# Middle feed-forwards of a two-layer decoder trunk: one group of columns, seven block products in the output projection, and some modulation dots beside the mixing stage

## The chip, the cores and the metric

The kernel runs as one launch on one core of a Trainium2 chip. The metric is the device time of a launch in microseconds (us). A core has five engines with their own instruction queues, each worked through in order: TensorE (PE, matmuls; its weight loads are listed as PEld), VectorE (DVE), ScalarE (ACT), GpSimd (POOL) and SyncE (SP). In this kernel SP issues the plain DMA loads and POOL the loads that add to what already lies in the destination, and the loads of the modulation weights. Matmul results land in PSUM; everything else lies in SBUF.

## The reference

The hidden state h has 512 tokens by 1024 features, in float32. There are two layers, and each is a half-step feed-forward, a mixing stage, and a second half-step feed-forward. Every one of the six stages begins with an RMS norm that is scaled and shifted by values made from a conditioning vector c, and ends with a residual that is gated by such values.

```python
c_act = silu(c)
for l in range(2):
    mod = c_act @ w_ada[l] + b_ada[l]          # 9 vectors of 1024: shift, scale, gate, three times
    hn = rms_norm(h, g_ffn1[l]) * (1 + sc1) + sh1
    gate, up = split(hn @ w_ffn1_in[l])        # 1024 -> 2 x 2816
    h = h + 0.5 * (1 + gt1) * ((silu(gate) * up) @ w_ffn1_out[l])    # 2816 -> 1024
    hn = rms_norm(h, g_mix[l]) * (1 + sc2) + sh2
    h = h + (1 + gt2) * (concat(attention, rwkv7, short_conv)(hn @ w_mix_in[l]) @ w_mix_out[l])
    # the second feed-forward is like the first, with w_ffn2_in, w_ffn2_out, sh3, sc3, gt3
```

## The kernel before

**Layout and precision.** h lies transposed: eight tiles `h[i]` of 128 features by 512 tokens. `HALVES` names the two halves of the tokens, `lo_` (0 to 255) and `hi_` (256 to 511). A product in float32 is made from three matmuls: each operand is split into a high part (`wH`, a cast on ACT, L104) and a low part (`wL`, the remainder, a subtraction on DVE, L105), and high times high, high times low and low times high are summed (`mm3`, `mm6`, `prod`). So each block of weights that PE multiplies costs ACT one cast and DVE one subtraction of the same size first. Four buffers each hold `wH` and `wL`.

**The order of the stages** is ffn1, mix and ffn2 of layer 0, then the same of layer 1 (`seq`, L1365). In this document the first feed-forward is ffn1 of layer 0, the *middle* ones are ffn2 of layer 0 and ffn1 of layer 1, and the *last* one is ffn2 of layer 1. All are made by `ffn` (L372), in these phases:

- *First tiles.* The first pairs of 128-wide columns of gate and up (two pairs, `n_first`; four in the first feed-forward) come from plain products with `w_in`.
- *Pairs* (`pair_in`, L483). Every further pair of columns is made by seven block products in place of eight, in the manner of Strassen and Winograd. Sums of quarters of hn (`P1`, `P2`, `T3`, `T4`, made in `whole` and `combine` beside the first tiles) meet sums of blocks of weights. The weight sums are made as follows: `S` is one block loaded by SP and a second added on top by a POOL load; DVE then adds block A(0,0) (`a11`, L497) and later subtracts, by sign, A(0,1) (L524); `S3`, the third pair sum, is A(0,0) loaded a second time into the tile `third` (L525) with A(1,0) added by a POOL load. Each product is 24 matmuls of 256 columns. Results are copied from PSUM to SBUF (`up`, `s1`, `s2`), added there (`gate` from `pG` and `s1`, L521), and put through silu and the product with up. The last product of a pair, `rest`, is done in the middle of the next pair.
- *Output product.* In the first and middle feed-forwards the 22 blocks of 128 inner columns go in two `GROUPS` of 12 and 10. After the pairs of each group come plain products with `w_out` over the group: 8 outputs of 128 features, 512 tokens wide, three matmuls each (L783); the last two outputs of the second group run by halves in `close` (L323), where the next stage's norm is worked in: `stats`, `spread` and `apply` of the lo half, then of the hi half, with the order on DVE and ACT written out by hand. The next stage's first three tiles start with the lo half.
- In the last feed-forward (`whole_k`) there is one group, and the output product itself is made by seven block products (`out_strassen`, L546): 42 `units`, seven products by six pieces of the inner columns; the gate is applied and h updated (L668) as each product ends, eight times four updates of 128 by 256.

**The modulation.** 128 columns of `mod` are still to be made when the first feed-forward starts (`todo`, L164). One such *dot* is a POOL load of 512 KB (L182) and one DVE instruction over 128 by 1024 (L168). `ada_steps` puts 48 of them into the first feed-forward, 36 into each middle one beside the output products, and the last eight go as half dots beside the pairs of the last feed-forward (`half_dots`, L705).

**The mixing stage** (`mix`, L803) projects hn into 20 tiles (`TILES`, in that order) and interleaves attention and two RWKV heads with these products by a hand-made budget of costs (`product_step`, L1315): a tile is finished, then live generators get their turn. Attention is live when tiles key to q3 are done, the first RWKV part when lo, k0, r0 and v0 are done. It makes no dots.

What the program's framework orders by itself (all but the blocks marked `manual_schedule`) follows program order as priority, and each tile name with a `tag` is a ring of `bufs` buffers: a new tile waits until the oldest one is no longer read.

## Time and profile before

| | us |
|---|---|
| median of 3 runs | 1888.41 (1885.57 to 1888.74) |
| the profiled execution's own time | 1883.92 |
| its span, first to last instruction | 1881.8 |
| first feed-forward, about | 0 to 376 |
| mix of layer 0, about | 376 to 625 |
| ffn2 of layer 0, about | 625 to 961 |
| ffn1 of layer 1, about | 961 to 1302 |
| mix of layer 1, about | 1302 to 1555 |
| ffn2 of layer 1, about | 1555 to 1882 |

The profile comes from one profiled execution, so sums are made against its own 1883.92 us, 2.1 us more than its span. Busy times of PE are modelled ends of pipelined matmuls; how fast PE really goes is read from the length of a stretch and the number of matmuls in it.

### The profile page before, as it was taken

To read this page: it belongs to the slowest core of one execution; us is meant where nothing else is said; L and a number is where in the kernel's file an instruction comes from. 1 tells how busy PE (TensorE), PEld (TensorE's weight loads), DVE (VectorE), ACT (ScalarE), POOL (GpSimd) and SP (SyncE) were. 2 spreads that over 40 slices of the span, in tenths; PEclk is the share of its full clock that TensorE was granted. 3 is DMA by queue.
4 is the path that set the end of the run, shared out by engine and by line. 5 is a ranking of instruction groups with operands and counts; after the bars stand their busy time and mean duration, and the time that the engine had idled before them with its cause. 6 is when DMAs were issued, how large, how long until landed. Compare 5 with 4: busy or idle time off the path is not lost.

```text
span 1881.8 us, 37923 instructions
## 1 busy us (share of the span) xinstructions
PE 1853.7 (99%) x15796; PEld 1733.0 (92%) x15796; DVE 1462.8 (78%) x2320; ACT 871.5 (46%) x1312; POOL 155.9 (8%) x243
## 2 busy tenths in 40 slices
PE   9999999999999999999999999999999999999999
PEld 8998899897889999899899989999878889999999
DVE  7787687858886877678787776878498768888996
ACT  4453355346432555245345524544554335555653
POOL 0101100100000010110100011110000000111120
PEclk9999999999999999999999999999999999999999
DMA  8667877521222285886817688782211315787855
GB/s 305 245 180 235 261 200 235 169 71 46 75 60 71 90 228 167 291 221 188 278 56 204 174 270 234 190 267 83 91 53 60 94 39 160 213 226 210 234 129 141
DMA packets 110028, 317.19 MB, mean 169 GB/s; under 512 B 23968, under 2 KB 29088, under 8 KB 108832
## 3 DMA queue, kind: packets, MB, share of 16 engines
q1 hardware_dynamic: 78192, 203.33, 31.6%
q0 software_dynamic: 31664, 111.43, 24.2%
q8 instruction: 124, 2.03, 0.4%
q14 instruction: 48, 0.39, 0.1%
HBM read 311.31 MB, written 3.41 MB: 167 GB/s over the span
## 4 chain that ended last, share of the span: by engine, by line
PE 83%; DVE 11%; ACT 2%; issue 2%; DMA 2%; SPq 0%; ACTq 0%; DVEq 0%
PE ps_mm L101 16%; PE ps_mm L94 8%; PE ps_mm L93 8%; PE ps_mm L95 8%; PE ps_d L467 7%; PE ps_d L469 6%; PE ps_d L468 6%; PE ps_f L469 3%; PE ps_f L467 3%; PE ps_f L468 3%; PE ps_d L661 2%; PE ps_g L469 2%; PE ps_g L467 1%; PE ps_g L468 1%; PE ps_f L661 1%
## 5 line engine op out<-in xcount | busy, mean ns | idle before, releaser
L104 ACT CAST wH<-wraw 128x1024 fp32r<-128x1024 f32 (+3 forms) x266 | 249.1, 940 | 402.0 <-PE ps_mm L94 102.2
L105 DVE TENSOR_TENSOR wL<-wraw,wH 128x1024 fp32r<-128x1024 f32 (+3 forms) x266 | 286.6, 1081 | 69.2 <-ACT wH L104 68.6
L467 PE MATMUL ps_d<-comH,wH 128*128 128x256 f32 x816 | 226.1, 277 | 1.2 <-ACT s L511 0.7
L468 PE MATMUL ps_d<-comL,wH 128*128 128x256 f32 x816 | 225.3, 276 | 0.0
L469 PE MATMUL ps_d<-comH,wL 128*128 128x256 f32 x816 | 225.2, 276 | 0.0
L93 PE MATMUL ps_mm<-actH,wH 128*128 128x512 f32 (+1 forms) x588 | 216.5, 368 | 0.0
L94 PE MATMUL ps_mm<-actL,wH 128*128 128x512 f32 (+1 forms) x588 | 216.0, 367 | 0.0
L95 PE MATMUL ps_mm<-actH,wL 128*128 128x512 f32 (+1 forms) x588 | 216.0, 367 | 0.0
L168 DVE SCALAR_TENSOR_TENSOR wada<-wada,crep 128x1024 f32<-128x1024 f32 (+1 forms) x148 | 169.4, 1162 | 48.1 <-DMA wada<-in_wadaT 47.8
L101 PE MATMUL ps_mm<-hnH,wL 128*128 128x256 f32 x976 | 199.5, 282 | 1.0 <-DVE wL L105 1.0
L101 PE MATMUL ps_mm<-hnH,wH 128*128 128x256 f32 x976 | 197.4, 282 | 0.6 <-ACT wH L104 0.3
L101 PE MATMUL ps_mm<-hnL,wH 128*128 128x256 f32 x976 | 197.2, 280 | 0.0
L104 ACT CAST wH<-sum 128x1024 fp32r<-128x1024 f32 x122 | 128.5, 1054 | 139.1 <-PE ps_d L468 66.4
L105 DVE TENSOR_TENSOR wL<-sum,wH 128x1024 fp32r<-128x1024 f32 x122 | 149.1, 1223 | 54.6 <-ACT wH L104 54.5
L101 PEld LDWEIGHTS ps_mm<-hnH,wL 128*128 128x128 f32 x976 | 149.5, 188 | 8.5 <-issue 6.6
L101 PEld LDWEIGHTS ps_mm<-hnH,wH 128*128 128x128 f32 x976 | 148.7, 188 | 8.5 <-issue 5.1
L467 PEld LDWEIGHTS ps_d<-comH,wH 128*128 128x128 f32 x816 | 153.2, 188 | 2.6 <-ACT s L511 1.7
L101 PEld LDWEIGHTS ps_mm<-hnL,wH 128*128 128x128 f32 x976 | 149.5, 188 | 5.2 <-issue 4.9
L468 PEld LDWEIGHTS ps_d<-comL,wH 128*128 128x128 f32 x816 | 153.2, 188 | 0.0
L469 PEld LDWEIGHTS ps_d<-comH,wL 128*128 128x128 f32 x816 | 153.2, 188 | 0.0
L95 PEld LDWEIGHTS ps_mm<-actH,wL 128*128 128x128 f32 x588 | 110.9, 189 | 18.3
L93 PEld LDWEIGHTS ps_mm<-actH,wH 128*128 128x128 f32 x588 | 110.9, 189 | 18.2
(474 smaller groups left out, 4716.4 us busy)
## 6 DMA issues: line engine op xcount, KB each, us to landing
wada<-in_wadaT POOLq DMA_DIRECT2D x120, 512.0 KB, 5.1
wraw<-in_wmi SPq DMA_DIRECT2D x40, 512.0 KB
wraw<-in_w2p SPq DMA_DIRECT2D x36, 512.0 KB
wraw<-in_w1p SPq DMA_DIRECT2D x32, 512.0 KB
wraw<-in_w1o SPq DMA_DIRECT2D x32, 384.0 KB
wraw<-in_w1i SPq DMA_DIRECT2D x20, 512.0 KB
wraw<-in_w1o SPq DMA_DIRECT2D x32, 320.0 KB
sum<-in_w2p SPq DMA_DIRECT2D x18, 512.0 KB
```

Source lines behind the costliest of these rows:

```text
L93: mm(acc, wH, xH, start=start, stop=False)
L94: mm(acc, wH, xL, start=False, stop=False)
L95: mm(acc, wL, xH, start=False, stop=stop)
L101: mm(acc[:, sl], w[a][:, k], x[b][:, sl], start=start and n == 0 and sl is HALVES[0], stop=stop and n == 2, skip_group_check=True)
L104: nc.scalar.copy(hi, src)
L105: return nc.vector.tensor_sub(lo, src, hi.bitcast(F32))
L168: stt(w, w, 1.0, crep, ALU.mult, ALU.mult, accum_out=out_)
L467: mm(pt[:, i], wH, x[k][0], start=start and i + k == 0, stop=False, skip_group_check=True)
L468: mm(pt[:, i], wH, x[k][1], start=False, stop=False, skip_group_check=True)
L469: last = mm(pt[:, i], wL, x[k][0], start=False, stop=k == 3, skip_group_check=True)
L661: mm(pt[m // 2][:, m % 2], w[:, 4 * k + m], x[:, y, k], start=start and u + k + n + m % 2 == 0, stop=u == NU - 1 and n == 2, skip_group_ch ...
```

## The change

The first feed-forward still runs `ffn`. The three others run a new function, `ffn_whole`; `ffn` loses what belonged to `whole_k`.

- One group of 22 blocks for all three; silu(gate) times up stays in float32 in `R` and is split only when it is used.
- In `pair_in` the third pair sum is made in place: `a00` is loaded once, used, and A(1,0) is then added onto it by a POOL load. From the second pair on, `pD` is copied into `pG` inside PSUM by ACT, and the product for the gate accumulates on top, so the addition of `gate` is gone. The product with the third sum is now the last of the pair.
- The output product is seven block products (`out_product`). Two of the results are carried from `pD` to `pG` by ACT copies, so h is updated six times four times; b is replaced by a minus b ahead of time. In the middle feed-forwards the sums of squares, the norm of the next stage and the loads of its first weights are worked into the last product, hi half first; `lead` makes the next stage's first tiles start with the hi half too.
- Dots: 16 in each mix, after tiles value to u0 (`MIX_DOTS`), with buffers of the second RWKV part's ring `u1`; 20 beside the pairs of each middle feed-forward and 8 beside those of the last one (`DOTS`), through four buffers that lie in the unused end of `R`.

```diff
+DOTS = ((0, 0, 2, 2, 2, 2), (0, 0, 3, 3, 3, 3, 2, 2, 2, 2))
+MIX_DOTS = {"value": 2, "q0": 2, "q1": 2, "q2": 2, "q3": 2, "lo": 1, "k0": 1, "r0": 1, "v0": 1, "c0": 1, "u0": 1}
+    def ada_plan(n, bufs, crow):
+        nc.sync.dma_start(crow, ins["crep"])
+        act(crow, crow, AF.Silu)
+        begun, left = {}, [n]
+        def dot(behind=None, pick=None):
+            l, i, k = todo.pop(0)
+            left[0] -= 1
+            w = bufs[pick if pick is not None else left[0] % len(bufs)]
+            nc.gpsimd.dma_start(w, ins["wadaT"][l, i, k])
...
+                ada_dot(mod[l, i][:, k : k + 1], w, crow)
...
             pts = [psum([P, T], "ps_mm", tag) for tag in ("mm", "mm", "r1")]
-            for sl in HALVES:
+            first_, second_ = lead[0]
+            lead[0] = HALVES
+            for sl in (first_, second_):
...
+    def ffn_whole(l, w_in, w_pair, w_s, hn, im, ss, need, then, ready):
...
+            R = [ap_.tile([P, 2, 2, T], F32, name="raw", tag="raw", bufs=NU) for _ in range(NU)]
+            spare = [R[-2][:, 0], R[-2][:, 1], R[-1][:, 0], R[-1][:, 1]]
...
+            def pair_in(p):
...
+                S = raw(A(1, 0), ("sum0", "sum1")[p % 2], after_="a00")
+                nc.gpsimd.dma_start(S, A(1, 1), accum_op=ALU.add)
...
+                prod(pF, S_, P1, True)
+                up = half_("up")
+                taken = nc.scalar.copy(up, pF)
+                a00 = raw(A(0, 0), ("first", "third")[p % 2], "a00")
+                prod(pD, hl(a00), B11, True)
+                s1 = half_("s1") if alone else pG
+                copied = nc.scalar.copy(s1, pD)
+                tt(S, S, a00, ALU.add)
+                nc.gpsimd.dma_start(a00, A(1, 0), accum_op=ALU.add)
...
+                third = hl(a00)
+                prod(pD, third, T3, False)
+                mark = tt(up, pD, up, ALU.add)
+                dots(mark)
+                tt(X[:, :, hi_], up, s2, ALU.mult)
+                mark = corner(X)
+                dots(mark)
...
+            def out_product(rest):
...
+                def weights(name, u):
+                    if name == "A3" and u >= NU - 2:
+                        w = ap_.tile([P, 2, KD, P], F32R, name="wHL", tag="raw", bufs=NU)
+                        pair = (w[:, 0], w[:, 1])
+                    elif name == "A3":
+                        pair = tuple(ap_.tile([P, KD, P], F32R, name=x, tag="com", bufs=8) for x in ("wH", "wL"))
...
+                def halves(name, u):
+                    a, d, b, c = parts(u)
+                    x = ap_.tile([P, 2, 2, H2], F32R, name="xs", tag="com", bufs=8)
...
+                plan = (("A0", "a", pD, True, ()), ("S", "a-c", pF, True, ((1, hi_, False),)), ("A1", "b", pG, False, ((0, lo_, True),)),
+                        ("S0", "-a", pD, False, ((0, hi_, False),)), ("S1", "c", pF, False, ((0, hi_, True),)),
+                        ("S3", "d", pD, False, ((1, hi_, True),)), ("A3", "b", pG, False, ((1, lo_, True),)))
...
+                        if q == 0 and u == NU - 1:
+                            for g in range(2):
+                                nc.scalar.copy(pG[g], pD[g])
...
+                    if t >= end - 2:
+                        prepare(t, 4)
...
+                with tc.manual_schedule(engines=HAND):
+                    sqs = []
+                    for t in range(end, len(units) - 2):
+                        for m in {0: (0, 1), 1: (2, 3)}.get(t - end, ()):
+                            sqs.append(update(5, m))
+                        prepare(t, 4)
+                        while sqs:
+                            total(sqs.pop(0), hi_)
+                        for _ in unit(t):
+                            pass
+                        if t == end + 1:
+                            stats(hi_)
+                            ahead(0, raws[0])
+                        if t == end + 2:
+                            spread(hi_)
+                            ahead(1, raws[1])
+                    apply(hi_, range(2))
+                    ahead(2, raws[2])
+                    apply(hi_, range(2, 5))
+                    k = 5
+                    for m in unit(len(units) - 1):
+                        sq = update(6, m)
+                        if k < KD:
+                            apply(hi_, range(k, k + 1))
+                            k += 1
+                        total(sq, lo_)
+                    stats(lo_)
+                    ahead(3, raws[3])
+                    spread(lo_)
+                    apply(lo_, range(KD))
+                    lead[0] = (hi_, lo_)
+                    return low_()
...
     def mix(l, hn, ss, mp, then, ready):
...
+            own = [U(1, n, [P, D]) for n in ("crow", "wada", "wada", "wada")]
+            dot = ada_plan(sum(MIX_DOTS.values()), own[1:], own[0])
             for name in TILES:
...
+                for _ in range(MIX_DOTS.get(name, 0)):
+                    dot()
```

## The prediction

> **What bounds the kernel now.** I read the page first: its busy line and the chain of work that ended last.

> ```profile
> PE 1853.7 (99%) x15796; PEld 1733.0 (92%) x15796; DVE 1462.8 (78%) x2320; ACT 871.5 (46%) x1312; POOL 155.9 (8%) x243
> PE 83%; DVE 11%; ACT 2%; issue 2%; DMA 2%; SPq 0%; ACTq 0%; DVEq 0%
> ```

> The chain says PE for 83% of the span; 11% is DVE, and that share has to be located. So next the windows view over the stretches that the change rebuilds. Columns: stretch, its length, then busy time and instructions of PE, PEld, DVE, ACT and POOL, granted clock, DMA share, GB/s.

> ```profile
> 743.40:808.70 65.30, 65.30 (x291) 54.08 (x290) 48.37 (x81) 14.94 (x19) 12.23 (x21) 1.00 0.83 271
> 904.90:945.80 40.90, 40.90 (x183) 33.88 (x182) 33.89 (x61) 15.56 (x24) 6.35 (x12) 1.00 0.79 266
> 945.80:961.30 15.50, 15.50 (x132) 15.50 (x131) 11.56 (x23) 5.87 (x11) 0.00 (x0) 1.00 0.00 1
> 961.30:1008.00 46.70, 45.69 (x393) 44.96 (x392) 39.38 (x64) 24.84 (x36) 2.02 (x3) 1.00 0.44 128
> ...
> 1084.20:1149.60 65.40, 65.40 (x292) 54.16 (x291) 46.20 (x79) 14.45 (x18) 11.53 (x21) 1.00 0.81 264
> 1245.80:1286.70 40.90, 40.90 (x183) 33.88 (x182) 35.62 (x63) 15.78 (x24) 6.36 (x12) 1.00 0.78 267
> 1286.70:1302.20 15.50, 15.50 (x132) 15.50 (x131) 9.89 (x20) 5.87 (x11) 0.00 (x0) 1.00 0.00 1
> 1595.70:1767.40 171.70, 171.70 (x1514) 171.70 (x1513) 141.30 (x181) 92.63 (x116) 25.03 (x34) 1.00 0.78 217
> 1767.40:1782.40 15.00, 15.00 (x135) 15.00 (x134) 12.47 (x22) 7.47 (x13) 0.62 (x1) 1.00 1.02 278
> 1782.40:1878.70 96.30, 94.30 (x794) 93.23 (x792) 78.97 (x124) 48.40 (x71) 15.79 (x19) 1.00 0.59 139
> ```

> Rows one to three are the plain output product of the first middle feed-forward, five to seven that of the second. The code gives 288 matmuls of 512 columns for 65.3 us, 227 ns each, and 180 for 40.9 us, also 227 ns. The pairs of the last feed-forward are 9 x 7 x 24 = 1512 matmuls of 256 columns in 171.7 us: 113.6 ns, half of 227. So PE is paid by the column, wherever the other engines keep up, and fewer columns mean less time. The last two rows are the seven block products as they run today in the last feed-forward: 15.0 + 96.3 = 111.3 us for 924 matmuls. The first of the seven, 132 matmuls in 15.0 us, goes at 113.6 ns; the other 792 at 121.6.

> **Output product of the middle feed-forwards.** Plain it is 22 x 8 x 3 = 528 matmuls of 512 columns, worth 1056 of 256; new it is 7 x 11 x 4 x 3 = 924, an eighth less, 132 x 113.6 ns = 15.0 us at equal pace. It takes today 65.3 + 40.9 + 15.5 = 121.7 us in layer 0 and 65.4 + 40.9 + 15.5 = 121.8 in layer 1. At best the new one takes 924 x 113.6 ns = 105.0 us (-16.7); as it runs in the last feed-forward, 111.3 (-10.4). What that loses has a source:

> ```profile
> its engine sat idle before it (us, times) until:
>   DVE wL L105: 3.2, 6
>   DVE h L668: 1.5, 2
> ```

> This is the view of the matmul line L661. 3.2 us wait for the low parts of weights. DVE has to make for each full unit of 24 matmuls (2.73 us of PE) a split of 1024 and one of 512, and in products S and S0 two more passes of 512. From the groups by shape:

> ```profile
> L105 DVE TENSOR_TENSOR wL<-sum,wH 128x1024 fp32r<-128x1024 f32 x122 | 149.1, 1223 | 54.6 <-ACT wH L104 54.5
> L606 DVE TENSOR_TENSOR sum<-sum,rowk 128x512 f32<-128x512 f32 x10 | 6.4, 680 | 0.0
> L668 DVE SCALAR_TENSOR_TENSOR h<-ps_d,cg,h 128x256 f32<-128x256 f32 x16 | 6.9, 475 | 2.0 <-PE ps_d L661 2.0
> L340 DVE TENSOR_TENSOR ss<-ss,sq 128x256 f32<-128x256 f32 x20 | 8.4, 421 | 4.4 <-ACT sq L215 4.2
> L104 ACT CAST xs<-xsum 128x512 fp32r<-128x512 f32 x10 | 6.1, 618 | 3.0 <-DVE xsum L634 3.0
> L258 DVE SCALAR_TENSOR_TENSOR hnL<-hn_t,mod,hnH 128x256 fp32r<-128x256 f32 x80 | 38.2, 478 | 0.9 <-ACT hnH L252 0.9
> ```

> S and S0 need 1.22 + 3 x 0.68 = 3.26 us per unit against 2.73: there DVE sets the pace. The change takes eight of the 32 updates (8 x 0.475 = 3.8 us) off DVE, four of them right behind the first product, where S is late; I put 0.8 us of the 3.2 back. Against it stand two things. First, the `com` ring has eight buffers, and `prepare(t, 4)` puts the third unit of A3 ahead of the second: two units hold three buffers each, two more hold the xs of S3, so the xs of the second unit waits until the first is multiplied; then an ACT pass of 0.62 and a DVE pass of 0.68 us stand alone: 1.5 us with their hand-overs. Second, the closing. Today the next stage's start loses 46.7 - 384 x 0.1136 = 3.1 us. New, DVE must do there, in written order, the splits of A3 (5.5 units x 1.90 = 10.5 us), eight updates (3.8), eight sums (3.4), three weight splits (3.7) and the hi norm (8 x 2 x 0.48 = 7.7), 29 us, beside 19 us of matmuls (A3 and the last 1.5 units of S3). But only 19 of the 29 must be done before the next stage's first tile: I take 1.0 us above today. Sum: 111.3 - 0.8 + 1.5 + 1.0 = 113.0 us, -8.7 in layer 0 and -8.8 in layer 1, together **-17.5 us**. Bounds: -16.7 each, and +2.7 each if the closing costs DVE's whole surplus of 10 us (9 above today's loss, rounded) and S and S0 lag in all their 11 units (11 x 0.53 = 5.8, where 3.2 is counted): 111.3 + 1.5 + 9 + 2.6 = 124.4.

> [...]

> **Pairs.** The number of products is unchanged, PE takes 171.7 us for nine pairs, and the question is whether anything else needs more than 19.08 us per pair. DVE after: nine passes of 1.22 (seven splits, two sums), four of 0.68, one of 0.42: 14.1 us; with three dots of 1.22 and their small read-outs 18.0 us, under 19.08, and only in four pairs of each middle feed-forward. Today's 141.3 of 171.7 hold half dots and ran without a stall. Transfers: the reload of A(0,0) goes, the dots come.

> ```profile
> q1 hardware_dynamic: 78192, 203.33, 31.6%
> q0 software_dynamic: 31664, 111.43, 24.2%
> third<-in_w2p POOLq DMA_DIRECT2D x18, 512.0 KB, 6.6
> L168 DVE SCALAR_TENSOR_TENSOR wada<-wada,crep 128x1024 f32<-128x1024 f32 x132 | 158.5, 1220 | 48.1 <-DMA wada<-in_wadaT 47.8
> ```

> Per MB, SP's queue takes 31.6% x 1881.8 / 203.33 = 2.9 us of all 16 engines and POOL's 4.1. A pair with three dots moves 4 x 0.52 MB on SP and 5 x 0.52 on POOL: 6.1 + 10.7 = 16.8 us of 19.08, 88%; the last feed-forward ran at 0.78, and its first block product at 1.02, without loss. The third sum's in-place add lands 6.6 us after its issue, which comes about 4 us into the pair; its product starts 16 us in. The adds and the dots' loads share POOL's queue, where a load waits for the dot four before it. So 0, bounds 0 and +4 us per middle feed-forward.

> **Last feed-forward.** Same pairs, four updates fewer behind the first product, -0.8, and the end wait of 1.5 on L668 stays: **-1.0 us**, bounds -3 and +1.

> **The mix.** Sixteen dots come in, 16 x 1.30 = 20.8 us of DVE per mix with their read-outs. What covers them? Windows over the end of the norm, the tiles value to q3, then lo to r0, then the stretch of the first RWKV part, in both layers:

> ```profile
> 376.00:397.00 21.00, 20.16 (x170) 19.37 (x169) 14.39 (x32) 12.68 (x23) 0.99 (x2) 1.00 0.10 33
> 397.00:416.00 19.00, 19.00 (x153) 16.64 (x151) 7.82 (x8) 7.76 (x12) 0.00 (x0) 1.00 0.42 139
> 416.00:448.00 32.00, 31.17 (x244) 27.06 (x244) 21.19 (x54) 19.89 (x54) 0.00 (x0) 1.00 0.16 53
> 448.00:497.00 49.00, 47.48 (x412) 38.02 (x412) 46.89 (x119) 24.58 (x64) 0.42 (x2) 1.00 0.20 60
> ...
> 1376.00:1425.00 49.00, 47.48 (x412) 38.01 (x412) 46.90 (x119) 24.59 (x64) 0.42 (x2) 1.00 0.20 60
> ```

> The first ten (13 us) meet 11 us of idle DVE and 6.6 in the 21 us before, so they are free. Those of lo, k0 and r0 meet another 11 us idle. Those of v0, c0 and u0 fall where DVE is full, and there the chain runs on DVE (start, length, what):

> ```profile
> 448.89 1.57 DVE P L1009 x8
> 451.12 3.26 DVE iP L1017
> 455.01 3.23 DVE rn L1018
> 458.89 1.15 DVE mx L1266 x2
> ```

> 3 x 1.30 = 3.9 us; one of them may slip before the chain starts, as v0's dot is ready first. I take **+3.0 us per mix, +6.0**. Bounds: 0 (all slip into gaps) and 20.8 per mix. The `crow` load and its silu are hidden in the first tiles: ACT was busy 7.8 of 19 us there. They bring table changes:

> ```profile
> L1275 ACT ACT_TABLE_LOAD x4 | 5.1, 1283 | 10.8 <-DVE mx L1269 10.7
> ```

> Two of 1.28 us. Without cover they would cost 2.6 us per mix.

> **Sum:** -17.5 - 1.0 + 6.0 = -12.5 us on the profiled execution: 1883.9 - 12.5 = 1871.4. The median of the three runs is 4.5 us above that execution, and what is measured next is a median: 1888.4 - 12.5 = **1876 us**.

> **Rivals.**
> *All hidden (0.20).* The mix hides every dot and the products lose only 4.5 us over 105.0, so 109.5 us: 2 x 12.2 + 1.5 = -26: 1862. For it: DVE has gaps in 416 to 448. Against: 46.89 of 49.
> *DVE takes over (0.22).* The closing and the S products give back half the gain: -8 - 1 + 6 = -3: 1885 (a closing 5 us longer per stage). For it: 29 us of DVE beside 19 of PE. Against: only 19 of the 29 come before the first hi tile.
> *Slower, by the mix (0.07).* DVE works in order, and a dot whose load is late holds all behind it (47.8 us of such waits in L168's row). If twelve of sixteen land on the path, 15.6 us per mix: 31.2 - 18.5 = +12.7: 1901. It turns at seven dots per mix, 18.5 / 2 / 1.30. Against: DVE idles 22 us in 397 to 448, and three buffers turn.
> *Narrow matmuls cost more (0.03).* The seven products would not save if one took 121.7 / 924 = 131.7 ns; then -1 + 6: 1893. For it no row; the slowest stretch, 121.6 ns with its waits, is short of it. [...]
> *Transfers bind in the pairs (0.03).* +4 each: 1884.

> **Chances.** The forecast has 0.45, between 1868 and 1884. Faster and slower count from 0.2% (3.8 us), about what a measurement of this kernel can tell: faster below 1884.6, slower above 1892.2. Faster: 0.45 + 0.20 and half of DVE taking over, 0.76; within 0.15; slower 0.09. The range leaves out the slow rivals, and the tail beyond "all hidden": **1861 to 1889**.

> **What would show it.** Right: the output product of each middle feed-forward in 111 to 115 us; PE at 113.6 ns through all pairs; the stretch from the value tile to the end of the first RWKV part 3 us longer. Wrong: idle PE ahead of A3's second unit or of the next stage's hi tiles beyond 3 us; pairs above 19.3 us; a mix longer by over 6 us.

## The result, and the profile after

The changed kernel is slower: **1944.28 us** (median of four, 1938.65 to 1953.61) against 1886.99 (1883.31 to 1888.74), ratio 1.0311, 95% interval 1.0267 to 1.0355. Forecast were 1876 and a range of 1861 to 1889. The profiled execution took 1953.61 us, its span 1951.9, so it is the slowest of the four; its span is 70.1 us longer than before, and these are to be found. (L numbers are now those of the changed kernel.)

PE has more instructions and more busy time, although it multiplies an eighth fewer columns in the middle output products:

```profile
PE 1865.5 (96%) x16468; PEld 1769.1 (91%) x16468; DVE 1539.1 (79%) x2432; ACT 930.5 (48%) x1422; POOL 191.4 (10%) x281
```

Where the time came from is read from windows over whole stages (columns as in the prediction; the granted clock is the number behind POOL). Of before: mix of layer 0, pairs of ffn2 of layer 0 in their two groups, the start of the mix of layer 1 up to the end of its first tiles, the mix of layer 1.

```profile
391.70:640.90 249.20, 240.40 (x2642) 211.98 (x2642) 189.16 (x389) 109.43 (x220) 0.85 (x4) 1.00 0.21 65
667.10:743.50 76.40, 76.40 (x675) 76.40 (x674) 58.31 (x62) 43.22 (x56) 6.77 (x9) 1.00 0.70 193
808.70:905.10 96.40, 96.24 (x842) 95.84 (x841) 72.71 (x78) 53.68 (x70) 7.70 (x10) 1.00 0.74 208
1302.20:1319.70 17.50, 17.47 (x152) 17.15 (x150) 12.49 (x34) 8.52 (x17) 1.01 (x2) 1.00 0.04 8
1319.70:1568.80 249.10, 240.30 (x2641) 211.88 (x2642) 189.11 (x389) 109.36 (x220) 1.93 (x6) 1.00 0.22 67
```

Of after: mix of layer 0; pairs, output product, and from its end to the next stage's block products, for ffn2 of layer 0; the same three for ffn1 of layer 1 (the third up to the end of the mix's first tiles); mix of layer 1; pairs of the last feed-forward. The stages overlap a little at these bounds: nine matmuls of the first of the seven products (1.1 us) lie in each window of pairs, and eighteen of the seventh (2.0 us) behind the window of the output product.

```profile
396.20:662.30 266.10, 246.10 (x2641) 215.86 (x2642) 208.49 (x425) 111.95 (x222) 7.71 (x17) 0.97 0.27 88
689.40:875.00 185.60, 178.73 (x1524) 177.77 (x1523) 148.37 (x184) 91.25 (x117) 25.44 (x36) 0.97 0.77 211
874.90:983.60 108.70, 105.72 (x907) 103.90 (x906) 90.55 (x141) 65.63 (x104) 16.57 (x19) 1.00 0.63 153
983.60:1044.00 60.40, 53.28 (x410) 51.61 (x411) 47.16 (x81) 27.01 (x40) 5.35 (x9) 0.92 0.43 141
1044.00:1229.30 185.30, 179.11 (x1523) 177.95 (x1523) 148.70 (x182) 91.30 (x116) 24.67 (x34) 0.97 0.77 211
1229.20:1336.50 107.30, 105.17 (x908) 103.80 (x906) 90.63 (x141) 65.42 (x104) 16.54 (x19) 1.00 0.63 154
1336.50:1370.20 33.70, 26.37 (x171) 24.46 (x170) 23.69 (x54) 14.31 (x27) 3.60 (x7) 0.85 0.32 114
1370.20:1628.90 258.70, 243.96 (x2641) 214.55 (x2642) 204.68 (x420) 110.34 (x221) 6.66 (x15) 0.98 0.27 87
1655.80:1838.20 182.40, 175.40 (x1523) 175.12 (x1522) 138.83 (x159) 91.50 (x116) 20.33 (x25) 0.98 0.68 178
```

| part | before | after | difference |
|---|---|---|---|
| pairs of the three feed-forwards | 172.9, 172.9, 171.9 | 185.6, 185.3, 182.5 | +36 |
| mix, layers 0 and 1 | 249.2, 249.1 | 266.2, 258.7 | +27 |
| output product alone, middle | 121.7, 121.8 | 108.8, 107.4 | -27 |
| from there to the next stage | 46.8, 17.6 | 60.5, 33.6 | +30 |
| the start of the program | 116.4 | 120.6 | +4 |

The table goes by bounds that are not rounded, so it can differ from a window by 0.1. The start, up to the first block product, is not part of the change; over all runs of this study with the new stages it took 116.7 to 120.6 us.

The seven products save 27 us in these bounds, and 21 when all 924 matmuls of each are counted (111.8 and 110.4 us). The stretch behind them gives it back, and pairs and mix, which were to cost 0 and 6 us, cost 63. The granted clock is 1.00 in every window of before and below it in every window here that grew.

**Pairs.** The groups by shape on DVE have the dots of the pairs (`raw`) and of the mix (`wada`). Behind the second bar stands the idle time of DVE ahead of them, and what ended it.

```profile
L170 DVE SCALAR_TENSOR_TENSOR raw<-raw,crow 128x1024 f32<-128x1024 f32 x48 | 58.5, 1221 | 44.0 <-DMA raw<-in_wadaT 41.1 <-ACT crow L200 2.8
L170 DVE SCALAR_TENSOR_TENSOR wada<-wada,crow 128x1024 f32<-128x1024 f32 x32 | 38.6, 1218 | 15.1 <-DMA wada<-in_wadaT 8.6 <-ACT crow L200 6.5
```

DVE stands 41.1 us for loads of the pairs' dots, and works in order. The timeline shows one such place, first on DVE, then on PE (start, length, what, in brackets the idle time and what ended it):

```profile
697.18 1.23 DVE L170 SCALAR_TENSOR_TENSOR raw<-raw,crow 128x1024 f32<-128x1024 f32 x1 [6.81 <-DMA raw<-in_wadaT]
...
698.67 1.22 DVE L107 TENSOR_TENSOR wL<-sum,wH 128x1024 fp32r<-128x1024 f32 x1
```

```profile
696.37 0.28 PE L711 MATMUL ps_d<-comL,wH 128*128 128x256 f32 x1
699.94 0.58 PE L712 MATMUL ps_d<-comH,wL 128*128 128x256 f32 x1 [3.30 <-DVE wL L107]
700.32 0.42 PE L710 MATMUL ps_d<-comH,wH 128*128 128x256 f32 x1
```

A dot waits 6.81 us, the split behind it is late, and PE stands 3.30 us. Then a matmul takes 0.42 us where it took 0.28: the granted clock, 1.00 up to 698.6, is 0.50 from there to 705.4. So a wait costs PE twice here: in the pairs of ffn2 of layer 0 it is 6.9 us of standing, and 4.4 us more for the matmuls that ran at half clock (10.2 us, PE standing in 1.4 of them). With the 1.1 us of the bounds that is 12.4 of the 12.7.

**The closing.** The same two views where the seventh product ends:

```profile
983.81 1.22 DVE L107 TENSOR_TENSOR wL<-wraw,wH 128x1024 fp32r<-128x1024 f32 x1
984.94 0.87 DVE L275 SCALAR_TENSOR_TENSOR hn_t<-h,gmod,ps_rstd 128x256 f32<-128x256 f32 x2
...
990.83 0.48 DVE L985 SCALAR_TENSOR_TENSOR h<-ps_g,cg,h 128x256 f32<-128x256 f32 x1
...
994.29 0.48 DVE L985 SCALAR_TENSOR_TENSOR h<-ps_g,cg,h 128x256 f32<-128x256 f32 x1 [1.85 <-PE ps_g L913]
```

```profile
982.74 0.85 PE L913 MATMUL ps_g<-xs,wHL 128*128 128x256 f32 x6
986.01 0.51 PE L95 MATMUL ps_mm<-hnH,wH 128*128 128x256 f32 x2 [2.42 <-ACT hnH L276]
```

The first of the last four updates of h (L985) runs 7.2 us after its matmuls are done (982.74 + 0.85, then 990.83), because the written order puts two weight splits and five applies of the hi half ahead of it. And PE stands although matmuls of the seventh product are left: the second group of a PSUM tile waits until the update has read the first (the update runs at 990.83, the next of these matmuls at 993.07). So the lo half's norm comes late too, and PE stands 2.01 us more at 1001.4.

**The mix.** The last RWKV head ends late; PE has by then used up its other work:

```profile
625.33 1.23 PE L103 MATMUL ps_mm<-yrH,wH 128*128 128x256 f32 x3 [3.74 <-DVE y L1480]
```

In all PE stands 20.0 us in this mix, 8.8 before, and the half clock costs 5.7 us more: together the 17 us.

### The profile page after: what moved, and what is told of

Its sections match the earlier page's. It is cut to its first block, busy times and chain, and to the rows that moved or that the text cites. A ratio compares the mean times of both kernels' runs of the same rounds, so it can differ in the third digit from the quotient of the medians.

```text
span 1951.9 us, 39617 instructions
## 1 busy us (share of the span) xinstructions
PE 1865.5 (96%) x16468; PEld 1769.1 (91%) x16468; DVE 1539.1 (79%) x2432; ACT 930.5 (48%) x1422; POOL 191.4 (10%) x281
## 3 DMA queue, kind: packets, MB, share of 16 engines
HBM read 315.50 MB, written 3.41 MB: 163 GB/s over the span
## 5 line engine op out<-in xcount | busy, mean ns | idle before, releaser
L106 ACT CAST wH<-wraw 128x1024 fp32r<-128x1024 f32 (+2 forms) x210 | 206.6, 988 | 332.6 <-PE ps_mm L103 58.4
L107 DVE TENSOR_TENSOR wL<-wraw,wH 128x1024 fp32r<-128x1024 f32 (+2 forms) x210 | 239.2, 1143 | 49.2 <-ACT wH L106 48.3
L107 DVE TENSOR_TENSOR wL<-sum,wH 128x1024 fp32r<-128x1024 f32 x159 | 194.5, 1223 | 56.3 <-ACT wH L106 55.7
L711 PE MATMUL ps_d<-comL,wH 128*128 128x256 f32 x648 | 183.5, 283 | 0.0
L103 PEld LDWEIGHTS ps_mm<-hnH,wL 128*128 128x128 f32 x976 | 149.2, 189 | 10.6 <-issue 5.1
L913 PE MATMUL ps_d<-xs,wH 128*128 128x256 f32 x792 | 135.4, 277 | 0.0
L913 PEld LDWEIGHTS ps_d<-xs,wH 128*128 128x128 f32 x792 | 119.4, 188 | 0.0
L913 PE MATMUL ps_d<-xs,wL 128*128 128x256 f32 x396 | 109.8, 277 | 3.4 <-DVE wL L107 3.4
L170 DVE SCALAR_TENSOR_TENSOR raw<-raw,crow 128x1024 f32<-128x1024 f32 x48 | 58.5, 1221 | 44.0 <-DMA raw<-in_wadaT 41.1
L913 PE MATMUL ps_f<-xs,wH 128*128 128x256 f32 x528 | 90.1, 276 | 0.0
L170 DVE SCALAR_TENSOR_TENSOR wada<-wada,crep 128x1024 f32<-128x1024 f32 x60 | 71.8, 1221 | 16.6 <-DMA wada<-in_wadaT 16.6
## 6 DMA issues: line engine op xcount, KB each, us to landing
wada<-in_wadaT POOLq DMA_DIRECT2D x80, 512.0 KB, 5.1
raw<-in_wadaT POOLq DMA_DIRECT2D x48, 512.0 KB, 7.2
wraw<-in_wmi SPq DMA_DIRECT2D x38, 512.0 KB
wraw<-in_w2p SPq DMA_DIRECT2D x36, 512.0 KB
wraw<-in_w1p SPq DMA_DIRECT2D x32, 512.0 KB
sum<-in_w2s SPq DMA_DIRECT2D x20, 512.0 KB
sum<-in_w2s POOLq DMA_DIRECT2D x20, 512.0 KB, 9.2
wraw<-in_w1i SPq DMA_DIRECT2D x18, 512.0 KB
```

Source lines behind the costliest of these rows:

```text
L103: mm(acc[:, sl], w[a][:, k], x[b][:, sl], start=start and n == 0 and sl is HALVES[0], stop=stop and n == 2, skip_group_check=True)
L106: nc.scalar.copy(hi, src)
L107: return nc.vector.tensor_sub(lo, src, hi.bitcast(F32))
L170: stt(w, w, 1.0, crep, ALU.mult, ALU.mult, accum_out=out_)
L711: mm(pt[:, i], wH, x[k][1], start=False, stop=False, skip_group_check=True)
L913: mm(pt[m // 2][:, m % 2], w[:, 4 * k + m], x[:, y, k], start=start and u + k + n + m % 2 == 0, stop=u == NU - 1 and n == 2, skip_group_ch ...
```

## The experiments

Theory 1: dots whose loads are late hold DVE's queue in pairs and mix. Theory 2: in the closing it is the written order, not the amount of work. Rivals: DVE simply has too much to do; the loads crowd the DMA engines. How much stages vary that a run leaves alone: pairs 179 to 187 us, mix 261 to 266 (layer 0) and 257 to 263 (layer 1), from the start of the seven products to the next stage 168 to 170 and 139 to 145.

**Pairs without loads, and without passes.**

```diff
-            nc.gpsimd.dma_start(w, ins["wadaT"][l, i, k])
+            if pick is None:
+                nc.gpsimd.dma_start(w, ins["wadaT"][l, i, k])
```

> The dots of the pairs keep their DVE pass over a whole tile, but its row of weights is not loaded (the modulation of the second and third feed-forward's dots is left out in value); mix and closing as in the changed kernel. Theory 1 (DVE, in order, stands at a dot whose load is late): the three stretches of pairs fall from 185.6, 185.3 and 182.5 us to 172 to 174 each, the whole by about 35 us. Rival A (the DVE passes themselves are too many): the pairs stay above 182 us. Rival B (the loads crowd the DMA engines): as theory 1 here; the next run tells them apart.

```diff
-                ada_dot(mod[l, i][:, k : k + 1], w, crow)
+                if pick is None:
+                    ada_dot(mod[l, i][:, k : k + 1], w, crow)
+                else:
+                    nc.vector.memset(mod[l, i][:, k : k + 1], 0.0)
```

> The loads of the pairs' dots stay, their DVE pass goes and nothing reads what is loaded (a one-column fill takes its place, so the modulation is left out in value). Theory 1: pairs 172 to 174 us, as nothing waits for the loads. Rival A (passes too many): also 172 to 174, but then the run without loads stays above 182. Rival B (the loads crowd the DMA engines, weights come late): pairs stay above 180.

Windows over the pairs, without loads (1916.37 us in all), then without passes (1933.89):

```profile
681.50:854.60 173.10, 173.10 (x1524) 173.03 (x1524) 147.08 (x180) 91.73 (x117) 16.38 (x19) 1.00 0.67 175
1024.00:1197.00 173.00, 173.00 (x1524) 172.93 (x1523) 146.93 (x179) 91.67 (x117) 15.52 (x18) 1.00 0.66 174
1627.80:1800.80 173.00, 173.00 (x1523) 172.92 (x1522) 135.41 (x154) 91.50 (x116) 16.33 (x19) 1.00 0.66 174
```

```profile
680.90:862.80 181.90, 175.17 (x1524) 174.90 (x1523) 129.47 (x157) 91.21 (x117) 23.49 (x33) 0.98 0.75 214
...
1646.40:1819.30 172.90, 172.90 (x1524) 172.82 (x1523) 130.32 (x147) 91.60 (x117) 17.98 (x22) 1.00 0.69 186
```

With all the passes and no load the pairs are back at 173.0 and the clock at 1.00: not the work, the loads. But without passes the middle pairs stay slow, which theory 1 did not expect. Each has one long wait of PE, 6.73 and 7.49 us, ahead of the product with the third sum. This is POOL, then ACT at the first of them:

```profile
707.85 1.28 POOL L749 DMA_DIRECT2D third<-in_w2p  x1
```

```profile
717.99 1.04 ACT L106 CAST wH<-third 128x1024 fp32r<-128x1024 f32 x1 [13.58 <-DMA third<-in_w2p]
```

The adding load of the third sum takes 10.1 us instead of the 6.6 of before; ACT, in order, stands at its cast, and the copy behind it that frees `ps_d` is late. Nothing holds the dots' loads back in this run, so they come in one burst (407 to 414 GB/s from 690 to 705 us). That rival is true as well, but for unpaced loads; in the changed kernel the dots pace them (POOL waits 164.4 us in all for a dot to free its buffer).

**Mix without dots, with the first ten, with the last six.** `dot()` leaves load and pass away for all sixteen, for the last six (the diff), and for the first ten (`< 6`).

```diff
+            kept_ = pick is not None or left[0] >= 6
+            if kept_:
                 nc.gpsimd.dma_start(w, ins["wadaT"][l, i, k])
...
+                if kept_:
                     ada_dot(mod[l, i][:, k : k + 1], w, crow)
```

> The sixteen dots of each mix are left out, loads and passes (crow, its load and its silu stay); pairs and closing as in the changed kernel. Theory 1: the mix of layer 0 goes from 266.2 to about 250 us and that of layer 1 from 258.7 to about 250 (before: 249.2 and 249.1), in all 25 us. Rival (the mix is longer because its start comes out of the new closing with late hi tiles, or because the crow silu changes tables on ACT): it stays above 257 in both.

> Of the sixteen dots of each mix the first ten (behind the tiles value to q3) stay, the last six (lo, k0, r0, v0, c0, u0) are left out, loads and passes. If the ten were free, as forecast, the mix takes 252 and 249 us (as without any dots). If the ten hold the chain, by waits for their loads and for crow and by delaying weight splits, 257 to 266 and 254 to 259.

> The other way round: the first ten dots of each mix are left out and the last six stay. If only the dots at v0, c0 and u0 cost, as forecast, 3 us more than without any: 255 and 252 us. If the ten are the cost, 252 and 249; if the six are, 262 and 257.

Windows over the two mixes, in this order of runs:

```profile
396.20:648.20 252.00, 241.76 (x2642) 212.38 (x2642) 189.72 (x389) 112.62 (x222) 0.84 (x4) 1.00 0.21 64
1355.20:1603.90 248.70, 240.48 (x2641) 212.12 (x2642) 189.40 (x389) 110.86 (x221) 0.84 (x4) 1.00 0.21 65
```

```profile
394.30:653.30 259.00, 246.14 (x2642) 215.50 (x2642) 200.90 (x413) 112.85 (x223) 4.54 (x11) 0.99 0.25 79
1358.90:1612.10 253.20, 242.06 (x2641) 213.45 (x2642) 196.73 (x404) 111.03 (x221) 2.91 (x8) 0.99 0.24 74
```

```profile
391.50:643.30 251.80, 241.28 (x2642) 211.83 (x2642) 196.17 (x402) 112.23 (x222) 2.43 (x7) 1.00 0.23 73
1339.10:1589.40 250.30, 240.17 (x2641) 211.75 (x2642) 192.87 (x399) 110.82 (x221) 1.37 (x5) 1.00 0.22 69
```

All sixteen dots cost 14.1 and 10.0 us, with the spread of the mix above 9 to 14 and 8 to 14. The ten that I had called free cost 7.0 and 4.5 alone; the six that I had priced cost -0.2 and +1.6 alone, within the spread. In that run all six passes of layer 0 were done within 15 us of the mix's start: nothing holds a dot in the mix, so the scheduler moves it up into DVE's idle time. In the changed kernel, too, all sixteen of layer 0 ran between 397 and 437, ahead of the RWKV chain (463). There the first stands 3.2 us for `crow`, four later ones 5.1 us in all for their loads through three buffers, and the splits behind them are late. The longest of the four:

```profile
416.15 1.23 DVE L170 SCALAR_TENSOR_TENSOR wada<-wada,crow 128x1024 f32<-128x1024 f32 x1 [2.79 <-DMA wada<-in_wadaT]
```

How much each of the two waits costs is not separated. With 2.9 us for `crow` and none for a load, six dots left the mix of layer 0 at 251.8 us, as without dots; with ten, 3.7 us for `crow` and 3.2 for one load, it took 259.0. No run took the loads alone out of the mix.

**The closing, in two steps.** First all four groups of matmuls ahead of the four updates; then the whole block in another order: hi updates and sums first, hi statistics after the first unit of the seventh product, the hi norm beside the others, the lo updates at once.

```diff
-                    for m in unit(len(units) - 1):
+                    for m in list(unit(len(units) - 1)):
```

> In the closing the four last groups of matmuls of the seventh product come ahead of the four updates, instead of each group behind the update of the one before. Theory 2 (the second group of a bank waits for the update of the first, and that stands in DVE's order behind five applies): the stretch from the end of the seventh product to the next stage's products falls from 60.5 to 50 to 53 us, and that into the mix from 33.6 to 23 to 26, in all 15 to 20 us. Rival (DVE has too much to do in the closing, 29 us beside 19 of matmuls): the wait moves to the lo half and the stretches, counted from the start of the seventh product, fall by under 3 us each.

```diff
+                    for m in range(4):
+                        sqs.append(update(5, m))
...
+                    run(6, (0,), range(4))
+                    stats(hi_)
+                    ahead(0, raws[0])
+                    run(6, (1,), range(4))
+                    spread(hi_)
+                    ahead(1, raws[1])
+                    apply(hi_, range(3))
...
+                    apply(hi_, range(3, KD))
+                    for m in (0, 2, 1, 3):
+                        run(6, (4, 5), (m,))
+                    for m in (0, 2, 1, 3):
+                        sqs.append(update(6, m))
```

> The closing is written anew: the four hi updates and their sums first, hi statistics after the first unit of the seventh product, hi norm during its other units, lo updates at once behind its last groups, the fourth weight split behind three of the lo applies. Theory 2 (order: the chain of update, sum, statistics and norm starts too late): from the start of the seven products to the next stage's products 169.2 becomes 155 to 160 us in layer 0, and 141.0 to the end of the mix's first tiles becomes 127 to 132 (ideal 148.6 and 121.3 at 113.6 ns). Rival (DVE's work in the closing is the bound, whatever the order): under 3 us less each, as with the four groups first.

Windows from the start of the seven products to the next stage's block products (layer 0) and to the end of the mix's first tiles (layer 1), of the second run:

```profile
861.90:1022.20 160.30, 154.31 (x1318) 151.62 (x1317) 137.08 (x221) 92.59 (x144) 21.76 (x27) 1.00 0.59 157
1205.90:1340.10 134.20, 126.73 (x1078) 124.29 (x1076) 113.26 (x194) 80.38 (x131) 19.91 (x26) 0.99 0.58 149
```

The first step gave 167.2 and 137.5 us, 2.0 and 3.5 less, far from the 15 to 20 expected in all: the wait went to the lo half, as the rival said. The second gave 160.3 and 134.2, 8.9 and 6.8 less, a little short of what was expected, with the same work on DVE (137.1 and 113.3 us, where the changed kernel has 137.7 and 114.3). So order it is, and one step of it is not enough.

**Pairs with early loads.** Each load is issued two dots ahead of its pass; no dot in the first pair.

```diff
+            def dots(behind):
+                p = at_p[0]
+                if p == n_first and not held:
+                    fetch(AHEAD)
+                if plan_[p]:
+                    plan_[p] -= 1
+                    dot_[0](behind, held[turn_[0]])
+                    turn_[0] += 1
+                    fetch()
```

> The dots of the pairs keep loads and passes, but each load is issued two dots ahead of its pass, and the first pair has none (three in each pair from the second product pair on, 20 in all; in the last feed-forward two). Theory 1 (DVE stands at late loads): pairs 173 to 176 us each, against 185.6, 185.3 and 182.5. Rival A (passes too many): above 180, as the passes are as many. Rival B (the loads crowd the DMA engines and hold the adding load of the third sum, seen as a single wait of 6.7 us in the run without passes): 177 to 182, with PE waiting at the third product.

174.7, 179.5 and 180.0 us: mended in one of three. In the last feed-forward a dot of a later pair ran at 1640.63, in the first pair, after a wait of 7.08 us. The code suggests why: the second dot of a pair is held behind `mark`, an instruction of ACT, and that does not hold an instruction of DVE. (No run changes this alone; the next changes it with the rest.) In ffn1 the waits (1.22 and 2.69 us of PE) lie in the last pairs, which have two buffers.

**All three together.** Every dot behind an instruction of DVE, its load two or three ahead; the new closing, with the lo updates ahead of the last three hi applies; twelve dots per mix, 24 per middle feed-forward.

```diff
-                mark = act(gate, gate if alone else pG, AF.Silu)
-                dots(mark)
+                act(gate, gate if alone else pG, AF.Silu)
+                dots(low[0])
...
-                    dot()
+                    dot(lows[0])
```

> The three parts mended together: in the pairs every dot is held behind an instruction of DVE itself (the second of each pair was held behind one of ACT, which does not hold DVE), its load two dots ahead, none at the start of the first pair, 24 per middle feed-forward; in the mix twelve dots, each held behind the weight split of its own tile, none before the tile q1; the closing in the new order, with the lo updates ahead of the last three hi applies and the fourth weight split behind all lo applies. If the causes are those found (late loads in front of in-order work, and order in the closing): pairs 173 to 176 us each, mix 250 to 255 each, from the start of the seven products to the next products 155 to 158 us in layer 0, the whole 1866 to 1878 us, faster than before (1888). Rival (the seven products and the dots need more of DVE than there is, whatever the order): above 1890.

> The same kernel with loads three dots ahead instead of two. If the transfer time of a load (about 7 us) is covered by two dots (over 10 us), no difference, within 3 us; if loads still come late, faster by 3 to 8 us; if more loads under way hold the adding loads of the sums, slower by 3 us and more.

1889.02 and 1884.73 us beside 1886.72: as fast as before, not the 1866 to 1878 expected. Two or three ahead differ by no more than 1.5 us in any stage but the start of the program (3.4). Pairs 173.0 us in all three feed-forwards, both times; from the seven products to the next stage 159 us in layer 0, where 155 to 158 were expected. What is left is the mix, expected at 250 to 255, here with three ahead:

```profile
390.90:647.40 256.50, 242.75 (x2641) 213.26 (x2642) 203.81 (x417) 111.35 (x222) 5.59 (x13) 0.99 0.25 84
...
1309.20:1570.20 261.00, 244.72 (x2641) 215.41 (x2642) 203.25 (x416) 112.36 (x223) 6.17 (x15) 0.97 0.27 88
```

Here no dot waits for its load. But the twelve, held to tiles up to v1, run until 488 in layer 0, and so also beside the RWKV chain, where DVE had no idle time to give (before, it was busy for 46.9 of the 49 us from 448 to 497).

**Fewer dots in the mix**: eight held, then six free.

```diff
-MIX_DOTS = {"q1": 1, "q2": 1, "q3": 1, "lo": 1, "k0": 1, "r0": 1, "v0": 1, "c0": 1, "u0": 1, "k1": 1, "r1": 1, "v1": 1}
+MIX_DOTS = {"q0": 1, "q1": 2, "q2": 2, "q3": 2, "lo": 1}
```

> As the kernel with loads three ahead, but each mix has eight dots instead of twelve, held behind the weight splits of the tiles q0 to lo, where DVE idles 11 of 20 us without dots; the pairs take four more (28 per middle feed-forward, three pairs with four). If the mix is longer by the dots that stand in the chain of the RWKV part (k0 to v1), it falls from 256.6 and 261.0 us to 250 to 253, the pairs stay at 173 to 175, the whole about 1872 to 1878 us. Rival (any dot in the mix costs its 1.3 us): 256 us still, and 1882 or more.

> As before it, but six dots per mix, held behind nothing, as in the run with the last six alone, and 30 per middle feed-forward, five pairs with four. Mix 250 to 252 us as there; if the pairs with four dots (14.1 + 4 x 1.30 = 19.3 us of DVE in 19.08 us) bind, each pair with four is 0.2 us and more longer, or waits appear: pairs 174 to 178. The whole 1870 to 1878 us; rival, transfers bind in the pairs with four: above 1882.

Both are a little faster than before, by 0.3 to 0.4%: 1877.45 us, ratio 0.9971 (0.9954 to 0.9988), and 1878.65, ratio 0.9964 (0.9949 to 0.9979). The mixes take 251.5 and 254.9 us with eight, 254.1 and 254.5 with six; only the first is within what was expected. The first middle pairs take 177.0 and 176.9, above the 173 to 175 expected with eight; PE stands 2.4 us in the last pair, which has one buffer for two dots.

**One dot in the last pair**, six early ones in the mix, 30 per middle feed-forward:

```diff
+DOTS = ((0, 0, 0, 2, 2, 2, 2), (0, 0, 2, 4, 4, 4, 4, 4, 4, 3, 1))
+MIX_DOTS = {"q0": 2, "q1": 1, "q2": 1, "q3": 1, "lo": 1}
```

> Six dots per mix behind the weight splits of q0 to lo, 30 per middle feed-forward, one in the last pair, where there is one buffer. If the wait of 3.19 us ahead of ps_q in layer 1 and of 2.36 and 1.64 us ahead of the last pair's third product came from dots whose loads were late in too few buffers, all three go, with the half-clock windows behind them: 4 to 8 us less than the run with eight dots, about 1869 to 1874 us. Rival (six pairs with four dots bind DVE, 19.3 us in 19.08): 1878 us and more, with waits inside the pairs.

1878.5 us against 1886.01, ratio **0.9957** (0.9940 to 0.9974), the lowest ratio, though its interval overlaps the other two. The median is above the 1869 to 1874 expected and where the rival put it, but the rival's sign, waits inside the pairs, is absent: pairs with four dots do not bind. The two waits ahead of the last pairs' third product are gone; that of 3.19 us in the mix of layer 1 is down to 1.37, with one window at half clock still behind it. Windows: mix of layer 0; pairs; seven products and closing, in both middle feed-forwards; mix of layer 1.

```profile
391.30:642.80 251.50, 241.67 (x2641) 212.25 (x2642) 196.60 (x403) 111.89 (x222) 2.43 (x7) 1.00 0.23 72
669.80:842.90 173.10, 173.10 (x1524) 173.03 (x1524) 159.98 (x209) 91.56 (x117) 29.88 (x44) 1.00 0.85 251
842.80:1001.50 158.70, 155.01 (x1317) 152.43 (x1317) 135.40 (x217) 92.34 (x144) 22.20 (x27) 1.00 0.61 163
1174.50:1304.80 130.30, 127.28 (x1077) 125.22 (x1075) 110.68 (x189) 77.89 (x128) 19.51 (x25) 1.00 0.57 143
1304.80:1558.20 253.40, 242.25 (x2642) 213.41 (x2642) 196.77 (x403) 113.07 (x223) 2.88 (x8) 0.99 0.24 78
```

**Waits of known length.** The second sum passes 3 to 8 times more through DVE in pairs 5 to 10 of the last feed-forward.

```diff
+                if ss is None and p > 4:
+                    for _ in range(p - 2):
+                        stt(S, S, 1.0, S, ALU.mult, ALU.max)
```

> The same kernel, and in the last feed-forward's pairs 5 to 10 the second sum passes 3 to 8 times more through DVE (1.22 us each, the value unchanged) before its split: waits of PE of growing length. If the granted clock goes to half for the next window of 3.41 us whenever PE idled for about half of one (over 1.9 us in all traces so far, and never under 1.1), each pair's wait under 1.4 us costs its own length alone, and each above 1.9 costs its length and 1.7 us more (3.4 us at half clock), 3.4 more where the idle time lies in two windows. Rival (the clock follows the mean load over a longer time): half clock for 7 us and more, or not at all.

In the first two of the six pairs the extra passes fitted, without a wait over 0.2 us. In the others the waits came out at 1.15, 2.14, 3.47 and 7.00 us (two of them in the fence), and the second fence has windows: the pairs, the stretch behind the wait of 1.15, and the stretches at half clock behind the other three.

```profile
1716.93 0.38 PE L714 MATMUL ps_d<-comH,wH 128*128 128x256 f32 x1 [2.14 <-ACT wH L108]
...
1772.40 0.58 PE L714 MATMUL ps_d<-comH,wH 128*128 128x256 f32 x1 [7.00 <-ACT wH L108]
```

```profile
1591.10:1789.90 198.80, 183.35 (x1525) 181.16 (x1525) 173.55 (x192) 91.09 (x117) 20.33 (x25) 0.96 0.64 169
1692.70:1700.00 7.30, 5.39 (x44) 5.18 (x44) 4.98 (x5) 3.97 (x5) 0.00 (x0) 1.00 0.13 38
1718.60:1722.00 3.40, 3.40 (x18) 3.40 (x18) 2.23 (x3) 1.04 (x1) 0.00 (x0) 0.50 0.17 40
1742.50:1749.30 6.80, 6.52 (x29) 6.22 (x30) 4.72 (x4) 2.21 (x4) 0.00 (x0) 0.50 0.22 77
1769.80:1776.60 6.80, 4.04 (x17) 3.75 (x18) 4.88 (x5) 2.63 (x3) 1.72 (x2) 0.50 0.77 188
```

None for 1.15, one window of 3.4 us for 2.14, two for 3.47, and two for 7.00. The 3.47 us lay almost wholly in one window, so the second was not expected. The stage is 25.7 us longer than 173.1: waits of 15.4 us in all (with the small ones), 7.0 us for the matmuls at half clock (half of the 17.1 us, without the 3.0 in which PE stood), and 3.3 that I don't account for.

## Why the prediction was wrong, step by step

- **Output product, -8.7 and -8.8 with its closing.** Measured in the same bounds (121.7 + 46.8 and 121.8 + 17.6 before; 108.8 + 60.5 and 107.4 + 33.6 after): +0.8 and +1.6, inside the bounds. The products themselves came out as forecast: all 924 matmuls took 111.8 and 110.4 us for 112.0 (113.0 without the closing's 1.0). The step that failed is "only 19 of the 29 must be done before the next stage's first tile: I take 1.0 us above today": it cost 11.7 and 14.0 (13.7 and 16.0 with the eighteen matmuls behind the bound). I counted what DVE has to do by then and not the order in which it is written, nor that two groups share a PSUM tile. The rival "DVE takes over" had the place and some 40% of the size (5 us), but its cause, too much work, is not it: the new order alone does the same work in 8.9 and 6.8 us less, and in the last version the two stretches are 158.7 and 130.3 us, 9.8 and 9.1 under before. The gain that was forecast is there; the written order held it.
- **Pairs, 0, with +4 as the bound.** +12.7, +12.4 and, in the last feed-forward, +10.6, where I had "same pairs" and -1.0 with a bound of +1. Of each, 1.1 us are the nine matmuls at the bound; the rest is the largest miss. The sum of DVE's work, 18.0 of 19.08 us, was right: with 30 dots, and four in six of the pairs, PE goes through without a stall, DVE at 160 of 173 us and the DMA engines at 0.85. What failed is that a sum of work has no term for waiting. The row that shows it, 47.8 us of DVE ahead of L168 for loads, I quoted and used in one rival only, for the mix. Those waits were harmless beside plain products (between 743.4 and 808.7 DVE stood some 7 us for such loads, and PE was busy for 65.30 of 65.30 us); beside the pairs a split for PE stands behind them. "Only in four pairs of each middle feed-forward" took it that a dot stays in its pair, and in the run with early loads one did not.
- **Mix, +3.0 each, with "the first ten free".** +17.0 and +9.6, within the bounds of 0 and 20.8. The split was the wrong way round: ten cost 7.0 and 4.5 alone, six nothing measurable, and none ran in the chain where I had priced three. The idle time of DVE that I set against the ten is real (with eight held dots the mix of layer 0 takes 251.5 us, as without any). What failed is again that the sum has no term for waiting: dots stood in that idle time, for `crow` and for their loads, with the splits behind them; how much each wait cost stays open.
- **The clock.** No step had it. After the start there are 14 stretches at half clock in the record of the granted clock, 71.7 us in all. PE worked in 62.9 of these, so they cost about 31 of the 70 us lost.
- **Rivals.** "Slower, by the mix" had the mechanism, a dot whose load is late holds all behind it, in one of its two places and without the clock: 1901. "Transfers bind in the pairs" did not happen in the changed kernel, only in the run with unpaced loads. "Narrow matmuls cost more" is out: 897 of the 924 matmuls took 108.7 us (of the 907 in the row eight belong to the norm), 121 ns each with their waits, where the rival needed 131.7.

## What to carry to other kernels

A load whose consumer stands in an in-order queue has to be issued a full transfer (here 7.2 us from issue to landing for the 512 KB of a dot in the pairs, the median) ahead of its place in that queue, with a buffer free for it, and its consumer has to be kept in its place, here by an instruction of the same engine; then even 92% of DVE (160 of 173 us in the pairs) is no limit here. Price what a moved step makes its engine *wait* for, not only its work, and ask what stands behind it in the new place. When the end of one stage is woven into the next by hand, move the longest chain (update, sum, statistics, norm) first; with the same work this was worth 7 to 9 us per stage here.
